# Head weights and convolved rows of an mLSTM mixer: their low-part subtractions on VectorE instead of GpSimd

## The chip, the cores and the metric

The kernel runs on one core of one Trainium2 chip. The metric is the device time of one execution in microseconds (us). Five engines take part, each with its own in-order queue of instructions: TensorE (PE: matmuls and transposes; its weight loads are shown as PEld), VectorE (DVE), ScalarE (ACT), GpSimd (POOL) and SyncE (SP), which here only issues DMAs. An instruction that waits holds up all that is queued behind it on its own engine.

## The reference, cut to what matters

Two layers of a residual network, each a mixer and an MLP, and then a third block of another kind, which the change does not touch. All is fp32, over 512 tokens of 1024 features. The mixer projects its input once and takes two branches. One is an mLSTM with four heads, whose q and k come from a 4-tap causal convolution of its input; the other is a gated 31-tap depthwise convolution.

```python
def mixer(h, w_in, w_conv_m, b_conv_m, w_q, w_k, w_v, ..., w_dw, b_dw, g_cn, b_cn, w_out):
    u = h @ w_in
    x_m, z, glu_a, glu_b = jnp.split(u, ...)                 # 4 x 1024 columns
    x_c = silu(causal_depthwise_conv(x_m, w_conv_m, b_conv_m))   # 4 taps
    q = einsum("bthd,hde->bthe", heads(x_c), w_q)            # 4 heads of 256
    k = einsum("bthd,hde->bthe", heads(x_c), w_k)
    v = einsum("bthd,hde->bthe", heads(x_m), w_v)
    ig, fg = gates from [q, k, v] @ w_gates
    h_m = mlstm_chunkwise(q, k * Dh**-0.5, v, ig, log_sigmoid(fg))
    h_m = sigmoid(z) * group_layer_norm(h_m, 4, g_mh)
    a = glu_a * sigmoid(glu_b)
    a = causal_depthwise_conv(a, w_dw, b_dw)                 # 31 taps
    a = silu(group_layer_norm(a, 8, g_cn, b_cn))
    return concatenate([h_m, a]) @ w_out
```

## The kernel before

Every large product is split in two parts so that it can run in the fast fp32r format of TensorE: a number x becomes its rounded value h and the difference lo = x - h, and a product is three matmuls, h·h, h·lo and lo·h (`mm3`, lines 164 to 166 of the profile). So each weight tile needs a DMA into `wr`, a cast to `wh` on ACT (line 155) and a subtraction that gives `wl` (the helper `sub`, line 143, which every subtraction of this kind shares). `sub` runs on VectorE unless its caller names another engine; `wunit` makes one weight tile, with three raw buffers and four of each part, and `unitsA` and `projA` make the tiles of a projection (128x1024 each) and pass the engine on. Activations are split in the same way.

A layer's mixer does its work in groups of 256 columns. The gated projections come first, and each group g ends by starting `taps(g)`: 60 VectorE instructions (line 589) that add 30 shifted products to two long PSUM banks, one bank for each half of the 256 columns, alternating between the two. ACT starts a bank (line 584) and copies it out at the end (line 593, into `cacc`). There are two such banks, so the four groups follow each other, and a group can only begin when the one before has been copied out. The taps are given a low priority when the program is built, so that they fill VectorE's gaps.

Then come the heads, four of 256 columns: `xproj(h)` projects x_m (two 128x1024 weight tiles), its consumer `xm_cons` splits the result into `xmh`, convolves it with 4 taps (`cv`, lines 633 and 636), gates it (line 640) and splits it into `xch` (cast on line 642, subtraction on line 643), and `qkv(h)` takes three 128x512 weight tiles (`wunit` on line 655) for v, q and k; ACT copies the results out of PSUM (lines 662 and 675). The heads are written in turn with `conv_norm(0)`, `conv_gate(0)` and `conv_norm(1)`, which work on finished convolution groups. After the gates comes the second half:

```python
        scores(0)
        zproj(2, 0)
        conv_norm(2)
        scores(1)
        numer(0)
```

`conv_norm(g)` transposes `cacc` of its group on TensorE (line 696) into the small transpose banks, of which there are two; ACT copies them back (line 697) and VectorE takes statistics (lines 700 and 701). `scores(h)` spreads a gate row over a transpose bank (line 819), multiplies q and k (line 827, into four of the four `mm` banks), takes exponentials on ACT (line 832), masks on POOL (line 834) and multiplies the two on VectorE (line 836), which frees an `mm` bank. `numer(h)` multiplies by v (line 851) into the next `mm` banks. Group 3's `conv_norm` is run inside the output projection.

The order on each engine is fixed when the program is built: a scheduler goes through the instructions as written, by priority and by when it thinks that each can run. On SP the order of the DMAs is written by hand.

Of the kernel before, what the change touches and what calls it, by code (L numbers as in the profile page):

```python
# [46 lines left out]
def fused_blocks_kernel(ctx: ExitStack, tc: tile.TileContext, I, out):  # L47
    nc = tc.nc
    V, S, P, PE, SP = nc.vector, nc.scalar, nc.gpsimd, nc.tensor, nc.sync
# [18 lines left out]
    def A(shape, dt=F32, name="a"):  # L68
        if not free_slots:
            raise RuntimeError(str(sorted(t.name for _, t in slot_of.values())))  # L70
        s = free_slots.pop(0)
        t = ap.tile(shape, dt, tag=f"A{s}", name=name)
        slot_of[id(t)] = (s, t)
        return t

    def HL(n, name):
        return A([128, 2, n], F32R, name)

    def free(*ts):
        for t in ts:  # L80
            free_slots.append(slot_of.pop(id(t))[0])
# [4 lines left out]
    def t2(shape, dt=F32, name="t2"):  # L86
        return t2p.tile(shape, dt, tag="t2", name=name)
# [4 lines left out]
    def mm():  # L92
        return mmp.tile([128, 512], F32, tag="mm", name="mm")
# [4 lines left out]
    def tr():  # L98
        return trp.tile([128, 512], F32, tag="tr", name="tr")
# [5 lines left out]
    def vv(name, i=0, n=None):  # L105
        o, w = VECS[name]
        return vec[:, o + i:o + i + (w - i if n is None else n)]
# [22 lines left out]
    def step():  # L130
        while pending:
            try:
                next(pending[0])
                return
            except StopIteration:
                pending.pop(0)
# [5 lines left out]
    def sub(dst, x_, h, eng=None):  # L142
        (eng or V).tensor_tensor(dst, x_, h.bitcast(F32), op=ALU.subtract)  # L143

    def wunit(src, a, b, eng=None, slots=False):

        raw = wrp.tile([128, a, b], F32, tag="wr", name="wr")
        SP.dma_start(raw, src)
        if slots:
            h = A([128, a, b], F32R, "wha")  # L150
            lo = A([128, a, b], F32R, "wla")
        else:
            h = whp.tile([128, a, b], F32R, tag="wh", name="wh")
            lo = wlp.tile([128, a, b], F32R, tag="wl", name="wl")
        S.copy(h, raw)  # L155
        sub(lo, raw, h, eng)
        step()
        return h, lo

    def unitsA(wv, c0, eng=None):  # L160
        return [wunit(wv[:, u * 4:u * 4 + 4, c0:c0 + 256], 4, 256, eng) for u in range(wv.shape[1] // 4)]

    def mm3(ps, ah, al, bh, bl, first, last):
        PE.matmul(ps, ah, bh, start=first, stop=False)  # L164
        PE.matmul(ps, ah, bl, start=False, stop=False)  # L165
        PE.matmul(ps, al, bh, start=False, stop=last)  # L166
# [69 lines left out]
    def mmA(ps, units, m, hT, view=lambda v: v, us=None):  # L236

        n = len(units)
        c = slice(m * 128, m * 128 + 128)
        for u in us or range(n):  # L240
            h, lo = units[u]
            for kk in range(4):
                kt = 4 * u + kk
                mm3(view(ps), h[:, kk, c], lo[:, kk, c], view(hT[kt][:, 0]), view(hT[kt][:, 1]),
                    kt == 0, kt == 4 * n - 1)

    def projA(wv, cols, hT, consumer, eng=None):

        ps = []
        for c0 in cols:  # L250
            un = unitsA(wv, c0, eng)
            pp = [mm(), mm()]
            for m in range(2):
                mmA(pp[m], un, m, hT)
            ps += pp
        consumer(ps)
# [315 lines left out]
    def mixer(l, pre, units, nxt, pre_next):  # L572
        wi = I["w_in"][l].rearrange("(k p) n -> p k n", p=128)
        wo = I["w_out"][l].rearrange("(k p) n -> p k n", p=128)
        hT = pre.hT
# [46 lines left out]
        def xm_cons(h):  # L622
            def fn(ps):
                xmh[h], xch[h] = [], []
                for m in range(2):
                    f = 2 * h + m
                    o = HL(512, "xmh")
                    S.copy(o[:, 0], ps[m])
                    sub(o[:, 1], ps[m], o[:, 0])
                    xmh[h].append(o)  # L630
                    cv = t2([128, 512], F32, "cv")
                    w0 = l * 32 + f * 4
                    act(cv, ps[m], AF.Identity, scale=vv("wcm", w0 + 3, 1), bias=vv("bcm", l * 8 + f, 1))
                    for j in (2, 1, 0):
                        s = 3 - j
                        V.scalar_tensor_tensor(cv[:, s:], ps[m][:, :512 - s], vv("wcm", w0 + j, 1), cv[:, s:],
                                               op0=ALU.mult, op1=ALU.add)
                    th = t2([128, 512], F32, "th")
                    act(th, cv, AF.Tanh)
                    V.scalar_tensor_tensor(cv, th, 1.0, cv, op0=ALU.add, op1=ALU.mult)  # L640
                    o = HL(512, "xch")
                    S.copy(o[:, 0], cv)
                    sub(o[:, 1], cv, o[:, 0], P)
                    xch[h].append(o)
            return fn

        def xproj(h):
            projA(wi, [256 * h], hT, xm_cons(h), eng=P)

        def qkv(h):  # L650
            wq = I["w_q"][l, h].rearrange("(k p) n -> p k n", p=128)
            wk = I["w_k"][l, h].rearrange("(k p) n -> p k n", p=128)
            wv = I["w_v"][l, h].rearrange("(k p) n -> p k n", p=128)
            for w, src, dst, nm in ((wv, xmh[h], vf, "v"), (wq, xch[h], q, "q"), (wk, xch[h], k, "k")):
                hh, ll = wunit(w, 2, 256, P)
                o = A([128, 2, 512], F32, nm)
                for m in range(2):
                    ps = mm()
                    for kt in range(2):
                        mm3(ps, hh[:, kt, m * 128:m * 128 + 128], ll[:, kt, m * 128:m * 128 + 128],  # L660
                            src[kt][:, 0], src[kt][:, 1], kt == 0, kt == 1)
                    S.copy(o[:, m], ps)
                dst[h] = o
                if w is wv:
                    free(*xmh[h])
            free(*xch[h])
            vt = A([128, 4, 257], F32, "v1")
            P.memset(vt[:, :, 256:257], 1.0)
            for b in range(2):
                bank = tr()  # L670
                for t in range(2):
                    for f in range(2):
                        PE.transpose(bank[:, t * 256 + f * 128:t * 256 + f * 128 + 128],
                                     vf[h][:, f, (2 * b + t) * 128:(2 * b + t) * 128 + 128], ident)
                S.copy(vt[:, 2 * b:2 * b + 2, 0:256], bank.rearrange("p (t e) -> p t e", t=2))
            v1[h] = vt
# [49 lines left out]
        def conv_split(g):  # L726
# [6 lines left out]
            free(cacc[g])  # L733

        xproj(0)
        xproj(1)
        qkv(0)
        xproj(2)
        qkv(1)
        conv_norm(0)  # L740
        xproj(3)
        free(glu[1])
        qkv(2)
        conv_gate(0)
        qkv(3)
# [686 lines left out]
```

## Time and profile before

| what | value |
|---|---|
| median of 3 runs | 2289.1 us (2287.65 to 2289.36) |
| the profiled execution | 2287.21 us, span 2285.2 us, mean granted clock 0.994 |
| busy: PE, DVE, ACT, POOL | 2240.0, 1530.7, 979.1, 301.3 us |
| mixer of layer 0, from its taps(1) to conv_norm(3) | 122 to 369 us |
| mixer of layer 1, the same | 869 to 1112 us |

The profile is of one execution. Its span begins with the first instruction and ends with the last. An engine's busy time is the sum of its instructions; an idle stretch is put down to the instruction of another engine that ended last before the engine went on. A row such as "265.02 4.49 DVE L589 ... x7" is a run of seven like instructions that starts at 265.02 us and lasts 4.49 us; it shows the shape of the first, and adjoining instructions overlap by some 0.08 us, so that costs are best taken from start to start.

### The profile page before, as it was taken

The page shows a single profiled execution, that of the slowest core. Times are in us where ns is not written, and L with a number is a line of the kernel's source. Part 1 is how long each engine was busy: PE and PEld are TensorE (multiplying, and loading weights), DVE is VectorE, ACT ScalarE, POOL GpSimd, SP SyncE. Part 2 cuts the span into 40 slices and gives each one's busy share as a digit, 9 for nine tenths or more (in the row PEclk, how much of TensorE's full clock was granted, in tenths as well). Part 3 has the DMA queues.
Part 4 walks back from the last instruction along what each step waited for, and adds up shares of the span by engine and source line. Part 5 has one row for each costly group of instructions (what it writes and reads, how often), then busy time and mean ns, then how long its engine had stood idle before and what let it go on. Part 6 is the DMA issues. An engine that isn't in the chain of part 4 may idle for free.

```text
span 2285.2 us, 29859 instructions
## 1 busy us (share of the span) xinstructions
PE 2240.0 (98%) x11164; PEld 1807.5 (79%) x11164; DVE 1530.7 (67%) x3037; ACT 979.1 (43%) x1651; POOL 301.3 (13%) x263
## 2 busy tenths in 40 slices
PE   8999999999999999999999999999999999999998
PEld 3777677878777888767887778888888888878886
DVE  4898998874555678899887643387566574652345
ACT  3557554543323334666543332235545554222232
POOL 1763000000000144400000000000321311000000
PEclk9999999999999999999999999999999999999999
DMA  7632134366565232321436544523211321532331
GB/s 265 211 116 79 55 120 131 128 198 194 179 190 176 87 117 85 92 65 47 148 120 187 177 127 127 170 75 114 88 50 54 98 77 60 172 95 94 99 131 65
DMA packets 194585, 277.69 MB, mean 122 GB/s; under 512 B 13812, under 2 KB 146548, under 8 KB 194440
## 3 DMA queue, kind: packets, MB, share of 16 engines
q1 hardware_dynamic: 194440, 275.78, 37.8%
q8 instruction: 88, 1.44, 0.3%
q14 instruction: 57, 0.47, 0.1%
HBM read 263.68 MB, written 14.37 MB: 122 GB/s over the span
## 4 chain that ended last, share of the span: by engine, by line
PE 74%; DVE 5%; ACT 2%; issue 1%; DMA 0%; POOL 0%; SPq 0%; DVEq 0%; ACTq 0%; POOLq 0%
PE mm L166 22%; PE mm L165 22%; PE mm L164 22%; PE cv L1129 1%; PE tr L1114 1%; PE mm L827 1%; PE mm L851 1%; PE mm L1093 0%; PE mm L1095 0%; DVE h L143 0%; PE tr L218 0%; DVE nt L176 0%; ACT sb L1103 0%; DVE h L231 0%; ACT junk L195 0%
## 5 line engine op out<-in xcount | busy, mean ns | idle before, releaser
L164 PE MATMUL mm<-h,wh 128*128 128x512 f32 (+1 forms) x1728 | 656.8, 381 | 3.8 <-DVE h L231 2.9
L165 PE MATMUL mm<-h,wh 128*128 128x512 f32 (+1 forms) x1728 | 654.3, 379 | 0.7 <-DVE h L143 0.6
L166 PE MATMUL mm<-h,wl 128*128 128x512 f32 (+1 forms) x1728 | 654.4, 379 | 0.1
L155 ACT CAST wh<-wr 128x1024 fp32r<-128x1024 f32 (+1 forms) x318 | 323.3, 1018 | 532.4 <-PE mm L165 249.7
L143 DVE TENSOR_TENSOR wl<-wr,wh 128x1024 fp32r<-128x1024 f32 x254 | 314.0, 1240 | 224.4 <-ACT wh L155 223.4
L164 PEld LDWEIGHTS mm<-h,wh 128*128 128x128 f32 x1728 | 324.7, 188 | 75.2 <-DVE h L231 6.8
L166 PEld LDWEIGHTS mm<-h,wl 128*128 128x128 f32 x1728 | 324.8, 188 | 68.3 <-issue 5.9
L165 PEld LDWEIGHTS mm<-h,wh 128*128 128x128 f32 x1728 | 325.3, 188 | 66.1 <-issue 3.0
L589 DVE SCALAR_TENSOR_TENSOR cv<-glu,vec,cv 128x511 f32<-128x511 f32 (+24 forms) x480 | 327.8, 732 | 7.1 <-ACT cv L584 6.8
L362 DVE SCALAR_TENSOR_TENSOR acc<-wr,csil,acc 128x1024 f32<-128x1024 f32 x91 | 116.1, 1284 | 127.6 <-DMA wr<-in_w_ada_dram 88.4
L165 PE MATMUL mm<-wl,hid 128*128 128x512 f32 x416 | 164.2, 395 | 0.0
L166 PE MATMUL mm<-wh,hid 128*128 128x512 f32 x416 | 164.1, 395 | 0.0
L164 PE MATMUL mm<-wh,hid 128*128 128x512 f32 x416 | 163.4, 395 | 0.0
L143 POOL TENSOR_TENSOR wl<-wr,wh 128x1024 fp32r<-128x1024 f32 (+1 forms) x68 | 137.8, 2033 | 185.0 <-ACT wh L155 144.4
L413 POOL PARTITION_BROADCAST G<-row x5 | 8.3, 1665 | 699.5 <-DVE row L410 383.4
L164 PEld LDWEIGHTS mm<-wh,hid 128*128 128x128 f32 x416 | 78.2, 188 | 19.9 <-issue 0.8
L166 PEld LDWEIGHTS mm<-wh,hid 128*128 128x128 f32 x416 | 78.2, 188 | 18.4
L165 PEld LDWEIGHTS mm<-wl,hid 128*128 128x128 f32 x416 | 78.2, 188 | 18.2
L543 ACT ACTIVATE s<-mm 128x512 f32<-128x512 f32 x64 | 38.0, 594 | 111.3 <-PE mm L166 111.3
L1103 ACT ACTIVATE sb<-sb,nm 128x512 f32<-128x512 f32 x64 | 46.4, 725 | 59.1 <-DVE nm L1101 50.2
L1083 POOL TENSOR_TENSOR bias<-band,amask 128x256 f32<-128x256 f32 x48 | 43.3, 910 | 206.5 <-DVE mx L1098 131.1
L546 DVE CAST hid<-s 128x512 fp32r<-128x512 f32 x64 | 29.0, 457 | 45.9 <-ACT s L544 45.9
(318 smaller groups left out, 3659.4 us busy)
## 6 DMA issues: line engine op xcount, KB each, us to landing
wr<-in_w_in_dram SPq DMA_DIRECT2D x140, 512.0 KB
wr<-in_w_ff_dram SPq DMA_DIRECT2D x128, 512.0 KB
wr<-in_w_ada_dram SPq DMA_DIRECT2D x80, 512.0 KB
wr<-in_w_out_dram SPq DMA_DIRECT2D x32, 512.0 KB
wr<-in_w_mod_dram SPq DMA_DIRECT2D x24, 512.0 KB
wr<-in_w_ada_dram SPq DMA_DIRECT2D x32, 256.0 KB
xd<-x SPq DMA_DIRECT2D x16, 512.0 KB
x<-xd SPq DMA_DIRECT2D x16, 512.0 KB
```

Of the source, the lines that this page charges most:

```text
L143: (eng or V).tensor_tensor(dst, x_, h.bitcast(F32), op=ALU.subtract)
L155: S.copy(h, raw)
L164: PE.matmul(ps, ah, bh, start=first, stop=False)
L165: PE.matmul(ps, ah, bl, start=False, stop=False)
L166: PE.matmul(ps, al, bh, start=False, stop=last)
L362: V.scalar_tensor_tensor(acc, raw, cv[:, kt:kt + 1], acc, op0=ALU.mult, op1=ALU.add)
L543: act(s, ps[m], AF.Relu)
L546: V.tensor_copy(o[:, 0], s)
L589: V.scalar_tensor_tensor(pa[m][:, s:], at[:, m, :512 - s], vv("wdw", l * 248 + (2 * g + m) * 31 + j, 1), pa[m][:, s:], op0=ALU.mult, op1=A ...
L827: PE.matmul(ps[:, :n], k[h][:, kt, j * 128:j * 128 + 128], q[h][:, kt, j * 128:], start=kt == 0, stop=kt == 1)
L1083: P.tensor_tensor(btile[:, b].rearrange("p (c r) -> p c r", r=8), bands[i][:, hh, :, o:o + 32].rearrange("p r c -> p c r"), amask[:, var, ...
L1103: act(sb, sb, AF.Exp, bias=nm, accum_out=sm)
```

## The change

Three calls no longer name GpSimd (`P`), so that VectorE does the subtraction:

```diff
-                    sub(o[:, 1], cv, o[:, 0], P)
+                    sub(o[:, 1], cv, o[:, 0])
...
         def xproj(h):
-            projA(wi, [256 * h], hT, xm_cons(h), eng=P)
+            projA(wi, [256 * h], hT, xm_cons(h))
...
-                hh, ll = wunit(w, 2, 256, P)
+                hh, ll = wunit(w, 2, 256)
```

In each of the two layers this is 8 subtractions of 128x1024 (`xproj`, two for each of four heads), 12 of 128x512 (`qkv`, three for each head) and 8 of 128x512 (`xch`, two for each head): 28 instructions. The other 28 subtractions of weights on GpSimd stay there. VectorE's order changes with it, since the low-priority taps now share it with more instructions of high priority.

VectorE's queue in layer 0, from the last instruction of `scores(0)` (w2_2409 is its tile) to the end of `taps(2)` (glu2_1020 is its input; cv_1028 is the first of its two banks, cv_1029 the second), stands before as:

```order
L836 SCALAR_TENSOR_TENSOR w2_2409<-mm_2434,w2_2409 128x128
L589 SCALAR_TENSOR_TENSOR cv_1029<-glu2_1020,vec_87,cv_1029 128x485
L589 SCALAR_TENSOR_TENSOR cv_1028<-glu2_1020,vec_87,cv_1028 128x484
L589 SCALAR_TENSOR_TENSOR cv_1029<-glu2_1020,vec_87,cv_1029 128x484
L589 SCALAR_TENSOR_TENSOR cv_1028<-glu2_1020,vec_87,cv_1028 128x483
L589 SCALAR_TENSOR_TENSOR cv_1029<-glu2_1020,vec_87,cv_1029 128x483
L589 SCALAR_TENSOR_TENSOR cv_1028<-glu2_1020,vec_87,cv_1028 128x482
L589 SCALAR_TENSOR_TENSOR cv_1029<-glu2_1020,vec_87,cv_1029 128x482
L589 SCALAR_TENSOR_TENSOR cv_1242<-glu3_1234,vec_87,cv_1242 128x511
```

Seven taps of group 2 stand behind `scores(0)`, and the first bank's last is the sixth of them. The same stretch of the changed kernel, its middle left out:

```order
L836 SCALAR_TENSOR_TENSOR w2_2409<-mm_2434,w2_2409 128x128
L589 SCALAR_TENSOR_TENSOR cv_1029<-glu2_1020,vec_87,cv_1029 128x500
L589 SCALAR_TENSOR_TENSOR cv_1028<-glu2_1020,vec_87,cv_1028 128x498
L589 SCALAR_TENSOR_TENSOR cv_1029<-glu2_1020,vec_87,cv_1029 128x499
...
L589 SCALAR_TENSOR_TENSOR cv_1029<-glu2_1020,vec_87,cv_1029 128x484
L589 SCALAR_TENSOR_TENSOR cv_1028<-glu2_1020,vec_87,cv_1028 128x482
L589 SCALAR_TENSOR_TENSOR cv_1029<-glu2_1020,vec_87,cv_1029 128x483
L589 SCALAR_TENSOR_TENSOR cv_1029<-glu2_1020,vec_87,cv_1029 128x482
L589 SCALAR_TENSOR_TENSOR cv_1242<-glu3_1234,vec_87,cv_1242 128x511
```

There are now 36 taps of group 2 in one run, with nothing between them; the first bank's last is the 34th. In layer 1 there are 33, with the first bank's last as the 32nd, where before there were 7 as well.

TensorE's queue at the same place of layer 0, behind `scores(0)` and `zproj(2,0)`, stands before as follows (q_1727 and k_1750 belong to `scores(1)`, cacc_1027 to `conv_norm(2)`, w1_2408 to `numer(0)`):

```order
L827 MATMUL mm_2545<-q_1727,k_1750 128x512
L696 MATMUL tr_2480<-ident_89,cacc_1027 128x128 x4
L827 MATMUL mm_2545<-q_1727,k_1750 128x512
L696 MATMUL tr_2498<-ident_89,cacc_1027 128x128 x4
L819 MATMUL tr_2540<-rp_2245,idr_104 128x512 x2
L827 MATMUL mm_2554<-q_1727,k_1750 128x384 x2
L827 MATMUL mm_2562<-q_1727,k_1750 128x256 x2
L827 MATMUL mm_2569<-q_1727,k_1750 128x128 x2
L851 MATMUL mm_2578<-v1_1594,w1_2408 128x257
```

And of the changed kernel:

```order
L827 MATMUL mm_2545<-q_1727,k_1750 128x512 x2
L827 MATMUL mm_2554<-q_1727,k_1750 128x384 x2
L827 MATMUL mm_2562<-q_1727,k_1750 128x256 x2
L827 MATMUL mm_2569<-q_1727,k_1750 128x128 x2
L696 MATMUL tr_2480<-ident_89,cacc_1027 128x128 x4
L696 MATMUL tr_2498<-ident_89,cacc_1027 128x128 x4
L819 MATMUL tr_2540<-rp_2245,idr_104 128x512 x2
L819 MATMUL tr_2662<-rp_2245,idr_104 128x512 x2
L851 MATMUL mm_2578<-v1_1594,w1_2408 128x257
```

All eight products of `scores(1)` now stand ahead of the transposes of `conv_norm(2)`; the gate rows of `scores(1)` and the first product of `numer(0)` still stand behind them. Layer 1 has the same change of order.

ACT's queue behind its copy of the first finished bank is, in the changed kernel of layer 0 (the names as above, w1_2543 of `scores(1)`):

```order
L593 COPY cacc_1027<-cv_1028 128x512
L584 ACTIVATE cv_1242<-glu3_1234,vec_87 128x512
L593 COPY cacc_1027<-cv_1029 128x512
L697 COPY cacc_1027<-tr_2480 128x512
L584 ACTIVATE cv_1243<-glu3_1234,vec_87 128x512
L697 COPY cacc_1027<-tr_2498 128x512
L832 ACTIVATE w1_2543<-tr_2540,bij_2394 128x128 x7
L832 ACTIVATE w2_2544<-tr_2540,bij_2394 128x128 x3
```

Before, both copies stood ahead of the first start of group 3's bank; the exponentials of `scores(1)` stood behind all of them then too.

## Rows read from the trace of the kernel before

**Rows 1.** The page: busy time and share of the span by engine.
```profile
PE 2240.0 (98%) x11164; PEld 1807.5 (79%) x11164; DVE 1530.7 (67%) x3037; ACT 979.1 (43%) x1651; POOL 301.3 (13%) x263
```
**Rows 2.** TensorE's waits, 0 to 420: waiter, awaited; total, times, longest (us).
```profile
PE mm L164 <- ACT v L662: 2.8, 1, 2.8
PE mm L164 <- ACT cg L730: 2.1, 1, 2.1
PE tr L696 <- ACT v L675: 1.6, 1, 1.6
```
**Rows 3.** Timeline of TensorE, layer 1's heads: start, length, instruction, idle before.
```profile
940.97 1.14 PE L696 MATMUL tr<-ident,cacc 128*128 128x128 f32 x8 [1.56 <-ACT v L675]
...
960.80 0.50 PE L164 MATMUL mm<-xch,wh 128*128 128x512 f32 x1 [2.21 <-ACT v L662]
```
**Rows 4.** GpSimd's groups by shape: busy us, mean ns, idle before and releasers.
```profile
L143 POOL TENSOR_TENSOR wl<-wr,wh 128x1024 fp32r<-128x1024 f32 x44 | 105.8, 2408 | 129.7 <-ACT wh L155 89.1 <-ACT wh L1314 40.3
...
L143 POOL TENSOR_TENSOR wl<-wr,wh 128x512 fp32r<-128x512 f32 x24 | 32.2, 1345 | 55.3 <-ACT wh L155 55.3
L143 POOL TENSOR_TENSOR xch<-cv,xch 128x512 fp32r<-128x512 f32 x16 | 20.7, 1292 | 20.7 <-ACT xch L642 20.7
```
**Rows 5.** VectorE's groups by shape, the same columns.
```profile
L143 DVE TENSOR_TENSOR wl<-wr,wh 128x1024 fp32r<-128x1024 f32 x254 | 314.0, 1240 | 224.4 <-ACT wh L155 223.4
...
L640 DVE SCALAR_TENSOR_TENSOR cv<-th,cv 128x512 f32<-128x512 f32 x16 | 18.8, 1172 | 2.1 <-ACT th L639 2.0
...
L143 DVE TENSOR_TENSOR xmh<-mm,xmh 128x512 fp32r<-128x512 f32 x16 | 11.0, 689 | 3.0 <-ACT xmh L628 3.0
```
**Rows 6.** Both mixers by windows: length, busy PE, PEld, DVE, ACT, POOL; clock, DMA.
```profile
122.00:369.00 247.00, 242.56 (x1102) 187.15 (x1102) 230.83 (x500) 141.00 (x264) 56.64 (x51) 0.99 0.32 99
869.00:1112.00 243.00, 239.17 (x1087) 185.70 (x1086) 222.37 (x490) 139.59 (x263) 51.33 (x47) 0.99 0.27 83
```
**Rows 7.** Timeline of VectorE near 181.
```profile
181.10 1.92 DVE L640 SCALAR_TENSOR_TENSOR cv<-th,cv 128x512 f32<-128x512 f32 x1
```
**Rows 8.** Timeline of GpSimd at that time.
```profile
180.05 2.41 POOL L143 TENSOR_TENSOR wl<-wr,wh 128x1024 fp32r<-128x1024 f32 x1 [1.94 <-ACT wh L155]
```
**Rows 9.** Timeline of VectorE behind scores(0), layer 0.
```profile
263.02 2.08 DVE L836 SCALAR_TENSOR_TENSOR w<-mm,w 128x512 f32<-128x512 f32 x4
265.02 4.49 DVE L589 SCALAR_TENSOR_TENSOR cv<-glu,vec,cv 128x485 f32<-128x485 f32 x7
...
274.24 0.69 DVE L836 SCALAR_TENSOR_TENSOR w<-mm,w 128x512 f32<-128x512 f32 x1
```
**Rows 10.** Timeline of ACT there.
```profile
268.92 0.59 ACT L593 COPY cacc<-cv 128x512 f32<-128x512 f32 x1 [4.49 <-DVE cv L589]
...
270.13 0.58 ACT L593 COPY cacc<-cv 128x512 f32<-128x512 f32 x1
```
**Rows 11.** Timeline of TensorE there.
```profile
259.42 4.58 PE L827 MATMUL mm<-q,k 128*128 128x512 f32 x16
...
269.44 1.02 PE L827 MATMUL mm<-q,k 128*128 128x512 f32 x2
...
275.48 0.60 PE L851 MATMUL mm<-v,w 128*128 128x257 f32 x2
```
**Rows 12.** Timeline of VectorE behind scores(0), layer 1.
```profile
1014.28 4.49 DVE L589 SCALAR_TENSOR_TENSOR cv<-glu,vec,cv 128x485 f32<-128x485 f32 x7
```
**Rows 13.** Timeline of ACT there.
```profile
1019.87 0.58 ACT L593 COPY cacc<-cv 128x512 f32<-128x512 f32 x1
```
**Rows 14.** Timeline of TensorE there.
```profile
1025.22 0.60 PE L851 MATMUL mm<-v,w 128*128 128x257 f32 x2
```
**Rows 15.** Timeline of TensorE behind its longest wait in layer 0's heads.
```profile
210.74 0.65 PE L164 MATMUL mm<-xch,wh 128*128 128x512 f32 x1 [2.82 <-ACT v L662]
211.19 0.63 PE L165 MATMUL mm<-xch,wh 128*128 128x512 f32 x1
...
214.49 0.40 PE L164 MATMUL mm<-xch,wh 128*128 128x512 f32 x1
214.72 0.39 PE L165 MATMUL mm<-xch,wh 128*128 128x512 f32 x1
```

## The prediction

> **What bounds the kernel now.** I read the busy shares first, then TensorE's waits by releaser in the two mixers, then VectorE's and GpSimd's groups by shape, then the mixers by windows, and last the timelines around one place. TensorE is busy for 98% of the span [rows 1], so the time falls only where TensorE waits, and rises by whatever makes it wait. In the first mixer and its surroundings it waits three times for more than a microsecond, 2.8, 2.1 and 1.6 us [rows 2]; in the second twice, 1.56 and 2.21 [rows 3]. The reader is to see that all five are put down to ACT, and none to GpSimd, whose instructions the change takes away. VectorE, at 67% over the span, is nearly full in the mixers alone: 230.83 of 247 us and 222.37 of 243 [rows 6], which leaves it 16.2 and 20.6 us idle.
>
> **What the change removes and adds.** On GpSimd each layer loses 8 subtractions of 2.41 us, 12 of 1.35 and 8 of 1.29 [rows 4], 45.8 us of an engine that nobody is seen to wait for: worth nothing by itself. On VectorE the same 28 cost less each. The 128x1024 one is 1.24 us [rows 5] and, with the overlap of 0.08 us between neighbours, 1.16 from start to start; the 128x512 one is not there for weights or for `xch`, but for `xmh` it takes 0.69 [rows 5], so 0.61: bounds are 0.61 (this row) and 1.35 (GpSimd's own), and I take 0.61, the nearer row being of the same engine, size and operation, although one input there lies in PSUM. Together 8 x 1.16 + 20 x 0.61 = 21.5 us per layer.
>
> Something comes back. Line 640 takes 1172 ns in the mean [rows 5] where an instruction of its size takes 0.69; the one at 181.10 took 1.92 [rows 7] and lay beside a GpSimd subtraction that ran from 180.05 to 182.46 [rows 8]. If all eight of a layer fall to 0.69, VectorE gains 8 x 0.48 = 3.9 us. So its load grows by 21.5 - 3.9 = 17.6 us per layer, against 16.2 and 20.6 us of idle time. By totals that nearly fits. It does not fit where it is put.
>
> The Trainium skill, GPSIMD Engine Reference, section 4.1 (Engine selection), would have elementwise work on VectorE; the rows agree on the price of one, 1240 against 2408 ns, and by that alone the sum would be a small gain, which is one of the rivals below. Its Perfetto Trace Analysis, section Optimizing Scalar/DVE Operations, speaks the other way: where DVE is saturated, offloading some work to other engines, GPSIMD included, may make sense, though shared reads may eat the gain. This trace has both sides, 230.83 of 247 us busy, and 1.92 us for one neighbour; by that rule the 17.6 us per layer outweigh the 3.9.
>
> **The place that pays.** VectorE's queue is in order. Its taps have low priority and are pushed back by the new subtractions, all of which stand in the head stage, ahead of `scores(0)`. That stage therefore does not grow on VectorE: 29 taps (19 us) of group 2 leave it, where 17.6 us come in, and I put its own effect at -1 us per layer, between +3 (VectorE now in the way of `xch`, which the products of `qkv` read) and -6 (the waits of 2.8 and 1.6 us and what follows them gone). The taps come back in one run behind `scores(0)`: 36 where there were 7 in layer 0, 33 where there were 7 in layer 1, by the order of the two programs.
>
> Layer 0: a tap takes 0.64 us (7 in 4.49 [rows 9]). Before, the first bank's last tap was the sixth, and ACT's copy of it followed at 268.92, having waited 4.49 us for it [rows 10]. Now it is the 34th: 28 x 0.64 = 17.9 us later, at 286.9. VectorE can't start the run earlier, since `scores(0)` stands ahead of it, and its four instructions wait for exponentials and products until 265.02 [rows 9]. The second bank's last tap ends at 265.0 + 36 x 0.64 = 288.1, and its copy ends at about 288.8 instead of 270.71 (270.13 + 0.58 [rows 10]): 18.1 us later.
>
> TensorE does all of `scores(1)`'s products first. They end at 269.44 + 4.58 = 274.0, the 4.58 being `scores(0)`'s sixteen rows [rows 11]. Then it stands before the transposes of `conv_norm(2)` until the first copy has ended, 286.9 + 0.6 = 287.5: a wait of some 13.5 us. It is not over then. The gate rows of `scores(1)` are behind these transposes on TensorE, its exponentials behind the copies on ACT, and the first product of `numer(0)` needs an `mm` bank, all four of which `scores(1)` holds until line 836 has run. Before, that line started 274.24 - 270.71 = 3.5 us after the second copy [rows 9, 10] and took 0.69. Now: 288.8 + 3.5 + 0.7 = 293.0 for line 851, which began at 275.48 [rows 11]. Layer 0 is 17.5 us late there.
>
> Layer 1: VectorE's run starts at 1014.28 [rows 12] and its 33 taps end at 1035.4. ACT's first copy comes a tap earlier, at 1034.8, then it starts group 3's bank (as in layer 0, some 0.7 us), and the second copy ends at about 1036.65 instead of 1020.45 [rows 13]; the same 3.5 + 0.7 puts line 851 at 1040.9 instead of 1025.22 [rows 14]: 15.7 us late. Nothing behind can make it up: from there to the end of `taps(3)` VectorE has the same instructions as before and is as late as TensorE.
>
> Each hole has a tail. After its wait of 2.82 us TensorE ran its next matmuls 0.41 us apart instead of 0.23, that is at about half of its clock (1.2 instead of 2.4 GHz), from 210.74 to 214.49 [rows 15]; eight or nine such cost 9 x 0.19 = 1.7 us. A wait five times as long is not in the trace; I take 1.7 again, with 0 (the transposes and VectorE set the pace there anyway) and 4 as ends.
>
> **Sum.** Layer 0: 17.5 + 1.7 - 1 = 18.2. Layer 1: 15.7 + 1.7 - 1 = 16.4. Together 34.6 us on the profiled 2287.2, so 2321.8. The median of the runs is 1.9 above the profiled execution: 2323.7, and I say 2324. Its own range: head stage +3 and tail 4 give 17.5 + 15.7 + 14 = 47.2, so 2336; head stage -6 and no tail give 33.2 - 12 = 21.2, so 2310.
>
> **Rivals.**
> *Waits are given back (2309 to 2314).* The hole is there, but TensorE's own waits go: 2.8, 1.6 and 2.1 in layer 0 and 2.2 and 1.6 in layer 1 [rows 2, 3], 10.3 us, with no tail: 33.2 - 10.3 = 22.9, so 2310.1 profiled and 2312. For it: a late TensorE finds ACT's results ready. Against: the first two of each layer come ahead of the hole.
>
> *VectorE's idle time takes it all (no change).* 17.6 us more against 16.2 and 20.6 idle [rows 6] leaves 1.4 us in layer 0 and none in layer 1: 2290.5. It needs taps that are spread out as before; the order has them in one run.
>
> *Faster, by GpSimd's lock and its slow subtractions.* If ACT's casts and `xch` wait for GpSimd, through the four buffers or through shared access to memory, more than the attribution shows, the head waits vanish: 2.8 + 1.6 + 2.2 + 1.6 = 8.2 us, and two tails of 1.7, 11.6 in all: 2277.5. This decides if VectorE reaches line 836 of `scores(0)` so early that its run of taps is over when TensorE wants the banks. For it: `xch` costs 0.69 instead of 1.29 on the way to the products. Against: line 836 needs what TensorE and ACT give it, at 263.
>
> *The whole added load lands on the path (upper side).* 21.5 us per layer, nothing returned: 2289.1 + 43 = 2332.
>
> **Chances.** The forecast 0.68, waits given back 0.14, no change 0.08, faster 0.06, whole load 0.04. This kernel's measurement can tell about 0.2%, 4.6 us, from no change. Faster: 0.06. Same: 0.08. Slower: 0.86. The range reaches from 2303, a little under the second case, to 2334, near the top of the first.
>
> **What would show it.** VectorE's timeline must show a single run of 36 taps behind the four line 836 of `scores(0)`, and 33 in layer 1; TensorE's waits must have a new first entry, line 696 for ACT's copy of line 593, twice, of 12 to 14 us, then a shorter one of 2 to 4 us at line 851 or 819; the mixer windows must end about 18 and 16 us later relative to their start, and the MLP's stay as they are. Line 640 should be near 0.69 us everywhere, and the 128x512 subtractions 0.6 to 0.7. If those waits are there but short, VectorE ran ahead and the sum is too big by what is missing; if the head stage is longer by more than 3 us, I have mispriced `xch` behind VectorE's queue; if no wait at line 696 is over 5 us, the forecast's mechanism is wrong.

## The result, and the profile after

The changed kernel takes 2315.84 us in the median (four runs, 2313.44 to 2316.89) against 2289.23 for the kernel before: 26.6 us more between the medians. The ratio of the means is 1.0113, with a 95% interval of 1.0096 to 1.0131. It is slower, as forecast, by some 8 us less than the 2324 predicted.

The page's first section, and TensorE's waits in the two mixers, first layer 0, then layer 1. As in [rows 2], its waits in the first 25 us, ahead of the mixer, are left out; they are 10.2 us before and 12.2 after, and the prediction's count of three waits does not have them:

```profile
PE 2243.0 (97%) x11164; PEld 1807.7 (78%) x11164; DVE 1561.8 (67%) x3093; ACT 982.1 (42%) x1651; POOL 211.1 (9%) x207
```
```profile
PE tr L696 <- ACT cacc L593: 13.1, 2, 12.8
...
PE mm L164 <- ACT cg L730: 2.1, 1, 2.1
PE mm L851 <- DVE w L836: 1.2, 1, 1.2
```
```profile
PE tr L696 <- ACT cacc L593: 12.3, 2, 12.0
PE mm L851 <- DVE w L836: 1.2, 1, 1.2
PE mm L164 <- ACT v L662: 0.8, 1, 0.8
```

The waits for `v` that [rows 2, 3] led with are gone or small (0.8 us is left in layer 1), and line 696 has a wait of 12 to 13 us in each layer that was not there. It is put down to ACT; ACT's own row tells whom ACT waited for. The place of [rows 9 to 11] in layer 0, VectorE, then ACT, then TensorE (start, length, instruction, idle before):

```profile
259.21 0.71 DVE L836 SCALAR_TENSOR_TENSOR w<-mm,w 128x256 f32<-128x256 f32 x2 [0.20 <-ACT w L832]
259.83 24.74 DVE L589 SCALAR_TENSOR_TENSOR cv<-glu,vec,cv 128x500 f32<-128x500 f32 x38
...
287.23 0.66 DVE L836 SCALAR_TENSOR_TENSOR w<-mm,w 128x512 f32<-128x512 f32 x1
```
```profile
281.59 0.59 ACT L593 COPY cacc<-cv 128x512 f32<-128x512 f32 x1 [15.86 <-DVE cv L589]
282.21 0.78 ACT L584 ACTIVATE cv<-glu,vec 128x512 f32<-128x512 f32 x1
282.98 0.59 ACT L593 COPY cacc<-cv 128x512 f32<-128x512 f32 x1
```
```profile
264.94 4.47 PE L827 MATMUL mm<-q,k 128*128 128x512 f32 x16
282.23 1.11 PE L696 MATMUL tr<-ident,cacc 128*128 128x128 f32 x4 [12.82 <-ACT cacc L593]
283.62 1.12 PE L696 MATMUL tr<-ident,cacc 128*128 128x128 f32 x4 [0.28 <-ACT cacc L593]
284.67 2.07 PE L819 MATMUL tr<-rp,idr 4*128 4x512 f32 x4
287.94 6.06 PE L851 MATMUL mm<-v,w 128*128 128x257 f32 x20 [1.21 <-DVE w L836]
```

The reader is to see one unbroken run of 38 taps (36 of group 2 and the first two of group 3), an ACT that stands 15.86 us before its copy, and a TensorE that stands 12.82 us before transposes that need the copy, and then again for line 836. Layer 1 has the same with 33:

```profile
1025.59 21.05 DVE L589 SCALAR_TENSOR_TENSOR cv<-glu,vec,cv 128x498 f32<-128x498 f32 x33
```
```profile
1046.68 1.12 PE L696 MATMUL tr<-ident,cacc 128*128 128x128 f32 x4 [12.04 <-ACT cacc L593]
...
1052.30 1.23 PE L851 MATMUL mm<-v,w 128*128 128x257 f32 x2 [1.17 <-DVE w L836]
```

VectorE's groups by shape answer to [rows 5]:

```profile
L143 DVE TENSOR_TENSOR wl<-wr,wh 128x1024 fp32r<-128x1024 f32 x270 | 333.4, 1239 | 222.3 <-ACT wh L155 221.3
...
L143 DVE TENSOR_TENSOR wl<-wr,wh 128x512 fp32r<-128x512 f32 x24 | 16.5, 689 | 1.2 <-ACT wh L155 1.0
...
L143 DVE TENSOR_TENSOR xch<-cv,xch 128x512 fp32r<-128x512 f32 x16 | 11.0, 689 | 0.5 <-ACT xch L642 0.5
...
L640 DVE SCALAR_TENSOR_TENSOR cv<-th,cv 128x512 f32<-128x512 f32 x16 | 11.0, 687 | 0.0
```

The prices were as assumed: 689 ns for the new 128x512 subtraction and 687 for line 640, down from 1172. The windows from the first copy of `taps(0)` to the first transpose of `conv_norm(3)`, before and then after (length, then busy time of PE, PEld, DVE, ACT, POOL):

```profile
120.50:369.30 248.80, 244.37 (x1111) 188.55 (x1110) 232.00 (x502) 142.47 (x267) 57.87 (x51) 0.99 0.32 100
867.70:1111.80 244.10, 240.27 (x1090) 186.59 (x1090) 222.92 (x491) 140.66 (x264) 51.89 (x48) 0.99 0.27 84
```
```profile
121.80:380.90 259.10, 244.11 (x1105) 188.38 (x1105) 248.14 (x530) 143.36 (x267) 13.59 (x23) 0.97 0.31 96
882.00:1139.00 257.00, 242.09 (x1091) 187.33 (x1090) 239.39 (x519) 141.09 (x264) 5.65 (x20) 0.97 0.26 79
```

VectorE has 16.1 and 16.5 us more to do (17.6 were forecast), and the mixers are 10.3 and 12.9 us longer. The spans of the two profiled executions differ by 30.0 us. The other 6.8 lie in stretches where nothing was changed: 1.3 ahead of the first window, 2.7 between the two and 2.8 behind the second. Between the two, TensorE has two waits in layer 0's MLP that it did not have before, 1.2 us for a cast (line 155) and 1.0 for line 531; e3 and e8 below take the old 498.4 us for this stretch. The 2.8 behind the second window are there in e1 and e9 too (1176.9 and 1176.4 us against 1173.4 before), but not in e3 (1173.3). Why is not shown.

### The profile page after: what moved, and what is told of

Same layout as the page of the kernel before. It is cut to its first block, busy times and chain, and to the rows that moved or that the text cites. A ratio compares the mean times of both kernels' runs of the same rounds, so it can differ in the third digit from the quotient of the medians.

```text
span 2315.2 us, 29852 instructions
## 1 busy us (share of the span) xinstructions
PE 2243.0 (97%) x11164; PEld 1807.7 (78%) x11164; DVE 1561.8 (67%) x3093; ACT 982.1 (42%) x1651; POOL 211.1 (9%) x207
## 4 chain that ended last, share of the span: by engine, by line
PE 84%; DVE 9%; ACT 3%; DMA 2%; issue 1%; POOL 0%; SPq 0%; DVEq 0%; ACTq 0%; POOLq 0%
PE mm L164 25%; PE mm L166 25%; PE mm L165 25%; DMA wr<-in_w_ada_dram 2%; DVE cv L589 2%; PE mm L851 2%; PE cv L1129 1%; PE tr L1114 1%; PE mm L827 1%; PE cv L439 1%; DVE h L143 1%; ACT cacc L711 1%; PE tr L218 1%; PE mm L1093 0%; PE mm L1095 0%
## 5 line engine op out<-in xcount | busy, mean ns | idle before, releaser
L143 DVE TENSOR_TENSOR wl<-wr,wh 128x1024 fp32r<-128x1024 f32 (+1 forms) x294 | 349.9, 1194 | 223.6 <-ACT wh L155 222.3
L589 DVE SCALAR_TENSOR_TENSOR cv<-glu,vec,cv 128x505 f32<-128x505 f32 (+28 forms) x480 | 327.2, 736 | 6.1 <-ACT cv L584 5.5
L362 DVE SCALAR_TENSOR_TENSOR acc<-wr,csil,acc 128x1024 f32<-128x1024 f32 x91 | 116.1, 1283 | 133.4 <-DMA wr<-in_w_ada_dram 93.8
L143 POOL TENSOR_TENSOR wl<-wr,wh 128x1024 fp32r<-128x1024 f32 x28 | 67.3, 2408 | 112.8 <-ACT wh L155 70.7
L546 DVE CAST hid<-s 128x512 fp32r<-128x512 f32 x64 | 28.1, 441 | 45.8 <-ACT s L544 45.7
```

Source lines behind the costliest of these rows:

```text
L362: V.scalar_tensor_tensor(acc, raw, cv[:, kt:kt + 1], acc, op0=ALU.mult, op1=ALU.add)
L546: V.tensor_copy(o[:, 0], s)
L589: V.scalar_tensor_tensor(pa[m][:, s:], at[:, m, :512 - s], vv("wdw", l * 248 + (2 * g + m) * 31 + j, 1), pa[m][:, s:], op0=ALU.mult, op1=A ...
```

## The experiments

Theory A is the prediction's: what stands in one run on VectorE behind `scores(0)` sets how late line 851 of `numer(0)` is. Theory B is the rival that only the amount of work given to VectorE counts, wherever it stands. Each kernel is compared with runs of the kernel before on the same chip.

**One part alone (e1 to e4).** Each part of the diff was applied by itself:

```diff
e1:  sub(o[:, 1], cv, o[:, 0])                  # xch alone
e2:  hh, ll = wunit(w, 2, 256)                  # qkv's weights alone
e3:  projA(wi, [256 * h], hT, xm_cons(h))       # xproj's weights alone
e4:  e2 and e3, xch stays on GpSimd
```

Expected: 

> Only the 16 subtractions of xch move to VectorE; the weights' stay on GpSimd. By its order 11 taps of group 2 stand behind scores(0) in layer 0 and 10 in layer 1 (7 before, 36 and 33 with the whole change). Theory A (the run of taps behind scores(0) sets the price: lateness of line 851 against scores(0) = 0.64 us x taps - 5.7, from 16.9 us for 36 and 16.1 for 33): 1.3 and 0.7 us, waits at line 696 under 3 us, time 2286 to 2291. Rival B (the added VectorE work sets the price, 26.6 us for 43.0): 16 x 0.61 = 9.8 us added, so +6: 2295. On the shorter heads: if what shortened them is xch itself, scores(0) comes 3 to 5 us earlier here too; if it is GpSimd's weight subtractions beside VectorE, it comes at its old time, 259.4 and 1009.2, and line 640 keeps instances of 1.3 to 1.9 us.

> Only the 24 weight subtractions of qkv (128x512) move to VectorE. By its order 15 and 12 taps of group 2 stand behind scores(0). Theory A: 0.64 x 15 - 5.7 = 3.9 and 2.0 us late, less what the heads gain (0 to 4): 2288 to 2295. Rival B: 24 x 0.61 = 14.6 us added, +9: 2298.

> Only the 16 weight subtractions of xproj (128x1024) move to VectorE, 8 in each layer, the same load in both. By its order 35 taps of group 2 stand behind scores(0) in layer 0 and 13 in layer 1. Theory A: 16.7 us late in layer 0 with a wait of 11 to 14 us at line 696, and 2.6 us in layer 1 with a wait under 4; less the heads' gain (0 to 5 a layer): 2299 to 2308. Rival B: 16 x 1.16 = 18.6 us added, +11.5: 2301, but half of it, 5 to 6 us, in each layer. The layers tell them apart, not the sum.

> All 40 weight subtractions of xproj and qkv move to VectorE; xch stays on GpSimd. By its order 28 taps behind scores(0) in layer 0 and 34 in layer 1. Theory A: 12.2 and 16.1 us late, so layer 0 has the smaller wait at line 696 (8 to 10 us) and layer 1 the larger (12 to 13), the reverse of the whole change; less the heads' gain (3 to 5 a layer): 2307 to 2314. Rival B: 33.2 us added, +20.5, the same in both layers: 2310. On the heads: if the weights' subtractions on GpSimd slowed line 640 and the weights, scores(0) comes 3 to 5 us earlier here as in the whole change.

Measured against 2287.3: e1 2293.51 (1.0028, 1.0015 to 1.004), e2 2289.34 (1.0012, 1.0002 to 1.0021), e3 2305.2 (1.008, 1.0065 to 1.0095), e4 2310.58 (1.0105, 1.009 to 1.012). e1 missed theory A's range by 2.5 us and lies nearer to theory B's 2295; there TensorE got two new waits of 3.4 us for line 636 in the heads. e2 lies in theory A's range and 9 us under B's 2298; the totals of e3 and e4 can't tell the two apart. The layers of e3 are the sharpest test, TensorE's waits in layer 0 and then in layer 1:

```profile
PE tr L696 <- ACT cacc L593: 13.6, 2, 13.4
```
```profile
PE mm L851 <- DVE w L836: 1.3, 1, 1.3
PE tr L673 <- ACT v L662: 1.2, 1, 1.2
PE tr L696 <- ACT cacc L593: 1.2, 1, 1.2
```

The same eight subtractions went to VectorE in both layers. In layer 0 they left 35 taps behind `scores(0)`, and TensorE waits 13.4 us; in layer 1 they left 13, and it waits 1.2. In layer 0 VectorE was idle for 17.5 us between the first copy of group 0 and the end of `scores(0)` (11.1 in the kernel before): it had the time for these taps and the order didn't use it. So the amount alone does not set the wait. In e4 the layers change places, as expected: 28 taps and 6.9 us for the longest wait (10.2 in two) in layer 0, 34 and 12.8 in layer 1. Over all kernels but e7, where `conv_norm(2)` is moved, and e10 and e11, where its transposes stand ahead of `scores(1)`'s products and 0 to 3 taps are left (there it is 11.6 to 12.7 us), the time from the end of `scores(0)`'s last line 836 to line 851 follows the number of taps of group 2 behind it:

| taps behind scores(0) | us from its end to line 851 | kernels |
|---|---|---|
| 6 to 8 | 10.4 to 11.4 | before, e6, e12 |
| 9 to 11 | 12.1 to 12.9 | e1, e6 |
| 12 to 15 | 13.3 to 16.4 | e2, e3, e5 |
| 27, 28 | 22.8, 24.6 | e9, e4 |
| 31 | 25.3, 25.3 | e8, e9 |
| 33 to 36 | 26.6 to 28.0 | after, e3, e4, e8 |

That is some 0.6 us for a tap, a tap's own time, from about 8 taps on.

The heads tell another thing. From the first copy of group 0 to line 827 of `scores(0)` it was 138.9 and 141.5 us before, 133.2 and 138.1 after; 139.4 and 142.0 with `xch` alone, 133.8 and 136.7 with the weights alone. What made the heads shorter was that GpSimd no longer did the weights. That taps left the head stage does not explain it: in e2, 8 and 5 of them left (5.1 and 3.2 us) while 7.3 us of subtractions came in, and the heads were 3.5 and 1.6 us shorter.

**The same work in another order (e5, e6).** The taps of group 1 get a higher priority, in the changed kernel and in e3:

```diff
-            with low(LOWP):
+            with low(600 if g == 1 else LOWP):
...
```

The cut part gives each tap and the two copies at the end the same number.

Expected: 

> The whole change, and the taps of group 1 given a higher priority (600 instead of 4000), so that groups 1 and 2 begin earlier on VectorE. Same instructions on every engine; by its order 14 taps of group 2 stand behind scores(0) in either layer instead of 36 and 33. Theory A (run of taps) with the idle time of VectorE's heads (6.7 and 11.5 us in the changed kernel) counted: line 851 3.3 us late in each layer instead of 16.9 and 16.1; the 22 and 19 taps put ahead (14.1 and 12.2 us) fill the idle time and lengthen the heads by the rest, 7.4 and 0.7: 2315.8 - 26.4 + 8.1 = 2297.5. Rival: the order alone made the loss, and nothing of the load has to be paid: 2289. Rival B (the added VectorE work sets the price wherever it stands): 2312 or more.

> Only xproj's 16 weight subtractions on VectorE, and the taps of group 1 given the higher priority (600). By its order 6 and 9 taps behind scores(0), instead of 35 and 13. Theory A: no lateness at line 851 in either layer (under 1 us), no wait at line 696 over 2 us; the heads keep the 3.6 and 2.4 us that they gained in the kernel with xproj alone, since VectorE had 17.5 and 9.3 us idle there and 29 and 4 taps (18.6 and 2.6 us) come in: 2287 - 6 + 1 = 2282, faster than the kernel before. Rival: the heads give the gain back to the taps: 2287 to 2290. Rival B (load): 2299.

Measured against 2287.79: e5 2313.42 (1.0104, 1.0087 to 1.0121), e6 2289.67 (1.0009, 1.0 to 1.0019). Both expectations of mine fell. In e5 the wait at line 696 did shrink, to 1.7 us in layer 0 and 3.1 in layer 1, but another came ahead of it. Its longest waits in layer 0, and what VectorE did just then:

```profile
PE mm L166 <- DVE wl L143: 12.3, 1, 12.3
```
```profile
192.47 7.66 DVE L590 SCALAR_TENSOR_TENSOR cv<-glu,vec,cv 128x487 f32<-128x487 f32 x12
...
203.32 1.19 DVE L143 TENSOR_TENSOR wl<-wr,wh 128x1024 fp32r<-128x1024 f32 x1
```

Twelve taps of group 1 (line 589 is 590 here) and the statistics of `conv_norm(0)` now stand ahead of a weight's difference that TensorE needs: 12.3 us, and 9.1 in layer 1. The loss moved and kept its size; 2313.42 is what theory B had (2312 or more). In e6, with less work on VectorE, 5.4 and 2.7 us of the same wait ate what the heads had gained, and the time is that of the kernel before, to 0.1%. Theory B had 2299 there. It is e3, at 2305.2, with its taps in another order: for this part of the change the order was the loss.

**The transposes later (e7).** `conv_norm(2)` is written after `scores(1)`, `numer(0)` and `zproj(2,1)`, and `conv_gate(2)` after `numer(1)`:

```diff
         zproj(2, 0)
-        conv_norm(2)
         scores(1)
         numer(0)
         zproj(2, 1)
+        conv_norm(2)
         scores(2)
+        numer(1)
         conv_gate(2)
-        numer(1)
```

Expected: 

> The whole change, with conv_norm(2) written after scores(1), numer(0) and zproj(2,1) and conv_gate(2) after numer(1), so that TensorE doesn't come to group 2's transposes so early. By its order 36 and 33 taps still stand in one run behind scores(0), ahead of line 836 of scores(1). Theory A: VectorE's in-order queue holds line 836 of scores(1) behind the run, so the wait moves from line 696 to line 851 and stays, 12 to 15 us in each layer: 2311 to 2316. Rival: the wait comes only from conv_norm(2)'s need of the finished banks; then it goes, and the time is 2283 to 2290.

Measured: 2315.49 (1.0118, 1.0103 to 1.0133). The size was as theory A had it, the place was not: line 696 still waits 8.9 us in layer 0 and 11.2 in layer 1, and in layer 0 waits of 3.8 us for a weight's difference and 3.5 for line 730 follow. Nor was the order as I had read it. In layer 0 only ten of the 36 taps stand in a run behind `scores(0)`, and line 836 of `scores(1)` is ahead of the others:

```profile
259.55 6.52 DVE L589 SCALAR_TENSOR_TENSOR cv<-glu,vec,cv 128x500 f32<-128x500 f32 x10
267.92 0.69 DVE L836 SCALAR_TENSOR_TENSOR w<-mm,w 128x512 f32<-128x512 f32 x1 [1.86 <-ACT w L832]
```

Line 851 is not late there (15.6 us behind line 827 of `scores(0)`, 16.1 in the kernel before). The other 26 taps stand among other instructions, most of them the small ones of `numer(0)`, and end at 292.1, and the transposes wait for them all the same. So the taps need not stand in one run to be waited for, and moving the one that waits did not help.

**GpSimd's work without its results (e8).** In the changed kernel GpSimd does the heads' 40 weight subtractions again, into a scratch tile that nothing reads:

```diff
         sub(lo, raw, h, eng)
+        if twice:
+            P.tensor_tensor(scr[-1][:, :a * b].rearrange("p (a b) -> p a b", b=b), raw, h.bitcast(F32), op=ALU.subtract)
```

Expected: 

> The whole change, and GpSimd does the 40 weight subtractions of the heads a second time, into a scratch tile that nobody reads: the same GpSimd work beside VectorE as before, and it holds the raw and cast buffers as before, but no product waits for its result. By its order 34 and 31 taps behind scores(0): 1.3 us less lateness in each layer than the changed kernel. Theory C (the heads were slowed by GpSimd working beside VectorE, and by the buffers that it held): line 640 goes back to 1.3 to 1.9 us for some, VectorE's own weight subtractions get longer than 1.24, and scores(0) is 3 to 6 us later after the last copy of group 0 than in the changed kernel (133.1 and 138.2 us): 2318 to 2326. Rival D (the heads were slowed because the products waited for GpSimd's slow results): the heads stay at 133 and 138: 2313 to 2316.

Measured: 2332.61 (1.0194, 1.0179 to 1.021), 16.8 us above the changed kernel and 6.6 above theory C's range. VectorE's groups there (line 640 of the other kernels is 644 here, line 636 is 640), and GpSimd's new one:

```profile
L143 DVE TENSOR_TENSOR wl<-wr,wh 128x512 fp32r<-128x512 f32 x24 | 22.3, 931 | 0.1
...
L143 DVE TENSOR_TENSOR xch<-cv,xch 128x512 fp32r<-128x512 f32 x16 | 19.1, 1195 | 0.1
...
L644 DVE SCALAR_TENSOR_TENSOR cv<-th,cv 128x512 f32<-128x512 f32 x16 | 13.6, 852 | 0.0
...
L640 DVE SCALAR_TENSOR_TENSOR cv<-mm,vec,cv 128x511 f32<-128x511 f32 x16 | 11.8, 739 | 0.0
...
L143 DVE TENSOR_TENSOR xmh<-mm,xmh 128x512 fp32r<-128x512 f32 x16 | 10.8, 678 | 0.5 <-ACT xmh L632 0.3
```
```profile
L160 POOL TENSOR_TENSOR scr<-wr,wh 128x1024 f32<-128x1024 f32 x16 | 47.0, 2935 | 20.1 <-ACT wh L157 19.7
```

Instructions of VectorE whose two large operands both lie in SBUF got longer (689 to 931 and 1195, 687 to 852 ns); those that read one of them from PSUM, `xmh` and the 4-tap convolution, did not (688 to 678, 746 to 739). GpSimd's own went from 2.41 to 2.94 us. The heads took 147.4 and 145.5 us instead of 133.2 and 138.1, with no product waiting for GpSimd. Together with the 128x1024 subtraction (1239 to 1285 ns in the mean of 270) the lengthened groups are 29.2 us longer; VectorE's idle time up to `scores(0)` took 11.8 of them, and the heads of both layers are 21.6 us longer. So GpSimd's work beside VectorE costs the heads time, and rival D is not needed for it. That GpSimd holds the raw and the cast tiles longer is in e8 too and was not tested by itself; the longer instructions leave some 4 us for it. How much of the gain of the change was the slow results all the same is not told apart by this kernel, in which VectorE has more to do than before.

**Taking work from VectorE again (e9 to e12).** `zproj`'s weight subtractions go to GpSimd, in the changed kernel (e9), with qkv's alone on VectorE (e10), and in the kernel before (e11); e12 is e10 with only `zproj(1)` and `zproj(2)`:

```diff
-                zu[h] = unitsA(wi, 1024 + 256 * h)
+                zu[h] = unitsA(wi, 1024 + 256 * h, P)
```
```diff
-                zu[h] = unitsA(wi, 1024 + 256 * h)
+                zu[h] = unitsA(wi, 1024 + 256 * h, P if h in (1, 2) else None)
```

Expected: 

> The whole change, and the 16 weight subtractions of zproj (128x1024, the gate z of the four heads) move the other way, from VectorE to GpSimd: 9.3 us less on VectorE in each layer. By its order 31 and 27 taps of group 2 still stand behind scores(0). Theory A (the run of taps in its place): lateness at line 851 falls by 0.64 x 5 and 0.64 x 6, 3.2 and 3.8 us: 2308 to 2310. Rival B (VectorE's load in the mixer sets the price): 9.3 us a layer less: 2296 to 2300.

> A version meant to beat both: only qkv's 24 weight subtractions move to VectorE (as in the kernel with qkv alone), and zproj's 16 go to GpSimd instead, so that VectorE has 7.3 - 9.3 us, less than before, in each layer, and what GpSimd does lies behind the heads. By its order 3 and 0 taps of group 2 behind scores(0). Theory A: no lateness at line 851, no wait at line 696 over 1 us; the heads keep the 3.6 and 1.6 us that qkv alone gave them, and part of the two halved-clock stretches goes: 2280 to 2284. Rival: GpSimd's new subtractions are waited for by zproj's products, or slow VectorE behind the heads: 2287 to 2292.

> The control of the run before: the kernel before with nothing but zproj's 16 weight subtractions moved to GpSimd. By its order no taps of group 2 stand behind scores(0). Theory A: TensorE did not wait for VectorE there, the heads' five waits for ACT stay: 2285 to 2289, no change. Rival (any relief of VectorE pays): 2280 to 2284.

> qkv's 24 weight subtractions on VectorE, and on GpSimd instead of them only the 8 of zproj(1) and zproj(2), which it meets ahead of the masks of scores(0) with time to spare; zproj(0), which stood among the xch there, and zproj(3), which stood ahead of the masks, stay on VectorE. By its order 8 and 6 taps of group 2 behind scores(0). Theory A: no wait for line 836 or for xch, lateness at line 851 under 1 us, the heads 3.6 and 1.6 us shorter than before as with qkv alone: 2281 to 2285, faster than before. Rival: what the heads gain is given back behind them, as in every version so far: 2287 to 2290.

Measured against 2288.49: e9 2316.26 (1.013, 1.0116 to 1.0144), e10 2292.67 (1.0024, 1.0014 to 1.0034), e11 2289.6 (1.0007, 0.9998 to 1.0016); against 2287.89: e12 2286.0 (0.9993, 0.9984 to 1.0002). e9 and e10 missed; e11 and e12 lie 0.6 and 1.0 us above theory A's ranges. VectorE, ACT and GpSimd of e9 ahead of line 836 of `scores(0)`, layer 0:

```profile
258.93 2.43 DVE L810 COPY bij<-cols 128x4 f32<-128x4 f32 x4
```
```profile
261.24 0.88 ACT L832 ACTIVATE w<-tr,bij 128x128 f32<-128x128 f32 x3 [3.25 <-DVE bij L810]
```
```profile
256.45 4.67 POOL L143 TENSOR_TENSOR wl<-wr,wh 128x1024 fp32r<-128x1024 f32 x2 [5.07 <-ACT wh L155]
261.68 0.29 POOL L834 TENSOR_SCALAR_AFFINE_SELECT w<-w 128x128 f32<-128x128 f32 x1 [0.56 <-ACT w L832]
```

The same four small copies in the kernel before:

```profile
260.70 0.36 DVE L810 COPY bij<-cols 128x4 f32<-128x4 f32 x4
```

Two subtractions of `zproj(3)` run on GpSimd just ahead of the masks of `scores(0)`. They do not hold up the masks: GpSimd is done and idle for 0.56 us (4.37 in layer 1) when the first mask's exponential comes. They hold up VectorE, whose copies beside them take 2.43 us instead of 0.36 (the first alone until 261.1, when the subtractions end), and the exponentials on ACT wait for these copies. In layer 1 it is line 724, with both operands in SBUF, that takes 5.1 us for two instead of 1.3, and ACT waits 7.35 us. So line 836 comes late; TensorE waits 3.2 and 5.6 us for it in e9, 4.5 and 4.8 in e10, and 3.2 and 4.4 in e11, where the first mask does come straight behind a subtraction.

Theory B had 9.3 us a layer coming back in e9, and nothing did. That does not speak against B, though: beside GpSimd the other instructions of VectorE got longer, and its busy time in the mixers is only 3.7 and 0.7 us below that of the changed kernel. From the end of `scores(0)` on, e9 follows the table. e12 takes out part of this (2.5 and 1.6 us of the wait are left) and is the fastest of all, but its interval reaches past 1: a version that beats the kernel before is not shown.

## Why the prediction was right, step by step

*The run of taps.* Right. It was to cost 17.5 us in layer 0 and 15.7 in layer 1 up to line 851, counted from `scores(0)`; from line 827 of `scores(0)` to line 851 it was 16.1 and 16.0 us before and 33.0 and 32.1 after, 16.9 and 16.1 more. The wait at line 696 was put at 13.5 us and is 12.82; the one at line 851, put at 2 to 4, is 1.2. The prices (0.61 for the 128x512 subtraction from start to start, 0.69 for line 640) held.

*The heads.* The sign was right and the size was not. I gave them -1 us per layer; they are 5.7 and 3.4 shorter. The term let the relief of VectorE and the taps that leave the head stage cancel against the 28 subtractions, and kept the end of TensorE's own waits there for its lower bound of -6. They went almost wholly: 0.7 us is left of TensorE's 4.4 us of idle time in layer 0's heads, 1.5 of 3.8 in layer 1's. The step behind it was that 45.8 us a layer of an engine that nobody is seen to wait for are worth nothing: the heads got shorter just where GpSimd was freed of weights (e2, e3, e4) and not with `xch` alone (e1). The faster rival had the heads nearly right (11.6 us by 8.2 of waits and two stretches of halved clock; 9.1 measured); what it lacked was the hole behind them.

*The tail of each hole.* I took 1.7 us, and a tail of nearly this size is there. TensorE's next matmul behind the twenty products of `numer(0)` in layer 0, before and after:

```profile
280.25 0.59 PE L164 MATMUL mm<-h,wh 128*128 128x512 f32 x1
```
```profile
293.65 0.59 PE L164 MATMUL mm<-h,wh 128*128 128x512 f32 x1
```

From the start of line 851 that is 4.77 us before, of which 0.42 is a gate product (line 819) of `scores(2)`, and 5.71 after, without it: 1.4 us more, and 1.5 in layer 1. It does not show at the end of the mixer: from line 851 to the transposes of `conv_norm(3)` it was 93.8 and 86.6 us before and 93.0 and 86.7 after, -0.8 and +0.1, because less stands there now. Two gate products went ahead of line 851 (0.8 us), and by the trace's records, of which a few can be missing, five matmuls in layer 0 and one in layer 1 (0.23 us each) went behind those transposes. The halved clock by windows of TensorE behind the hole of layer 0 (granted clock in the third column from the end):

```profile
282.20:288.00 5.80, 4.28 (x13) 2.58 (x13) 5.66 (x23) 5.20 (x14) 0.59 (x2) 0.50 0.00 1
288.00:293.60 5.60, 5.60 (x19) 4.70 (x20) 4.70 (x17) 4.19 (x16) 1.74 (x6) 0.74 0.00 0
293.60:340.00 46.40, 46.40 (x211) 36.74 (x210) 44.48 (x132) 28.44 (x60) 1.67 (x4) 1.00 0.30 92
```

After its 12.82 us of standing, TensorE has half of its clock (1.2 GHz) for 5.8 us and 0.74 in the mean of the 5.6 us behind; the first of these windows lies ahead of line 851, inside the first term.

*The sum.* 16.9 - 5.7 - 0.8 and 16.1 - 3.4 + 0.1 make 23.2 us in the mixers where I had 34.6, 11.4 too much. The rest up to the 26.6 of the medians (3.4 us) lies outside the mixers, where I had put nothing and expected the MLPs to stay as they are; the cause is open. So the total is nearer than its terms by luck: an error of 11.4 us met one of 3.4 the other way.

*The rivals.* "Waits are given back" was the nearest, at 2312, nearer than my own 2324, and partly true: the waits that went are those of the heads, ahead of the hole, with GpSimd's work and not because TensorE came late; the one for line 730 (2.1 us), behind the hole, stayed. "VectorE's idle time takes it all" is what e2, e6 and e12 come near to with less work moved. With all of it moved, VectorE's idle time in the mixers fell only from 16.8 and 21.2 us to 11.0 and 17.6, in pieces where it mostly waits for ACT. "The whole added load" is out: 16.1 and 16.5 us came on VectorE, not 21.5.

*Open.* e3 and e6 show that an order can lose 13 us where VectorE has idle time to spare. For the whole change it is not told apart whether the order or the amount sets the price: e5 takes 14 taps behind `scores(0)` instead of 36 and 33 and loses as much elsewhere, e7 loses as much too. Whether some order would make the whole change free was not found in these two, and is not shown to be impossible.

## What to carry to other kernels

When work is moved to an engine with idle time, look where its queue puts what it already had: low-priority work that was spread out comes back as one run, and the run's length times one instruction is the wait. Count the run in the order of the built program, from the last instruction that must precede it to the first that somebody waits for; that gave 17.5 and 15.7 us against 16.9 and 16.1. It prices the order that is built, and does not say that another order would be free (e5, e7). And where the helper engine is emptied, price what it did to its neighbours as well as what it did itself; where it is given work, price what that will do to them (e9).

## What the runs showed of the hardware

GpSimd and VectorE slow each other when both read two large operands from SBUF: in e8 a 128x512 subtraction on VectorE went from 689 to 1195 ns in the mean and GpSimd's 128x1024 one from 2408 to 2935. With one operand in PSUM VectorE was not slowed (688 and 678 ns). The Trainium skill, SBUF — State Buffer, section Who interferes with whom, states just this of VectorE instructions with two SBUF inputs and GpSimd instructions that read SBUF, and these runs agree; that GpSimd's are lengthened as well has its number here, 2408 to 2935 ns. I had priced only line 640 for this. In the change as a whole the heads got shorter when GpSimd was freed of the weights; how much of that is this slowing is not told apart.

A copy can be held up too: in e9 four copies of 128x4 on VectorE took 2.43 us beside a subtraction on GpSimd, and 0.36 in the kernel before.
